# A decoder trunk on one core: the two-operand work of GpSimd moves to VectorE

## The chip, the core and the metric

The kernel runs on one core of a Trainium2 chip. A core has five engines with instruction queues of their own that run in order and wait for each other through semaphores: TensorE (PE in the profile; PEld are its weight loads), VectorE (DVE), ScalarE (ACT), GpSimd (POOL) and SyncE (SP), which here only issues DMA transfers. The metric is the time of one execution on the device in microseconds (us); smaller is better. Before the change the median of three runs is 1664.11 us (1661.08 to 1664.7).

## What is computed

One layer of a hybrid decoder on 1024 tokens of 1024 features, in float32: a mixer with two groups (a causal convolution of width 31 with layer norm, and an RWKV-7 recurrence with 8 heads of 64), cross-attention into 256 memory tokens, and a SwiGLU feed-forward of 2816. Each is wrapped in RMS norms before and after. Cut to the parts that the change touches:

```python
def conformer_conv(u, conv_w, conv_b, ln_g, ln_b):
    h = u[..., :D_CONV] * jax.nn.sigmoid(u[..., D_CONV:])
    h = lax.conv_general_dilated(h, conv_w[:, None, :], window_strides=(1,),
        padding=[(CONV_WIDTH - 1, 0)], ..., feature_group_count=D_CONV) + conv_b
    return jax.nn.silu(layer_norm(h, ln_g, ln_b))

def rwkv7_recurrence(r, w, k, v, kk, a):
    def step(S, inp):
        r_t, w_t, k_t, v_t, kk_t, a_t = inp
        s_kk = jnp.einsum("bhvk,bhk->bhv", S, kk_t)
        S = (S * w_t[:, :, None, :] - s_kk[..., None] * (kk_t * a_t)[:, :, None, :]
             + v_t[..., None] * k_t[:, :, None, :])
        return S, jnp.einsum("bhvk,bhk->bhv", S, r_t)
    ...

def swiglu(h, w_gu, w_down):
    gu = h @ w_gu
    return (jax.nn.silu(gu[..., :D_FF]) * gu[..., D_FF:]) @ w_down
```

## The kernel before

The tokens go through in two blocks of 512, called pass 1 and pass 2 here. Every large product is done in three matmuls (`mm3`, L192): an operand x is split into a rounded part hi and a remainder lo, and hi x hi, hi x lo and lo x hi are summed. Weights come in blocks of 128x1024 (`wload`, L169): SP loads the raw block, ACT rounds it (whi, L166), and DVE or POOL subtracts (wlo, L167). One block feeds 24 matmuls of up to 512 columns. `feat` (psf in the profile) makes feature-major results, `tokmajor` (pst) token-major ones.

The recurrence is done in chunks of 64 tokens, eight to a block. `rwkv_prep` (L417) makes the factors of every head pair. `rwkv_inverse` (L587) inverts unit triangular 64x64 matrices: for the 32x32 diagonal blocks of all chunks and heads at once it takes 31 steps, each a product into tm (L616) and an addition into Tt (L617) over rows 0 to t and columns t+1 to 31. Rows under 20 (`cut`) are POOL's, the others DVE's. Then the result goes through DRAM into TT, and PE completes the blocks (psx, and pst at L643). `rwkv_chain` (L647) goes through the eight chunks one after the other: psp (PE), a copy (ACT), psu (PE), uv (ACT), pss (PE), the new state Sn (DVE, L701) and from it the uv of the next chunk (DVE, L705); psq and psy beside them make the output. After every second chunk `rwkv_out` (L720) normalises it and stores it; the mixing projection (`mix_out`, L809) reads it from DRAM, rounds it (ACT) and subtracts (DVE).

The convolution (`conv_taps`, L336) works on four groups of 128 channels; a tap is one multiply-and-add of 128x512 on DVE (L351), 30 for each group. Group 0 is different: ACT scales the shifted input (tap, L348) and POOL adds (L349).

The convolution and the state chain of a pass stand beside other work for PE: in pass 1 the products of the memory (`memory_maps`, with psgm and psvw) and the input projection of the second block, in pass 2 the feed-forward of the first block. In the source they are generators that are woven together; the order on each engine, however, is made by a scheduler that goes by a timeline of its own and may place an instruction ahead of others wherever its operands allow. Once placed, an engine's queue runs in that order.

In the code the steps of the prediction can be followed at L165 to L182 (lo parts; `pool_share` gives POOL every second or third weight block of some stages), L336 to L354 (taps), L506 to L510 and L547 (three products of the preparation), L607 to L617 (the inverse), L645 (TT), L684 to L713 (the chain), L922 (the last feed-forward's scaling).

Of the kernel before, what the change touches and what calls it, by code (L numbers as in the profile page):

```python
# [9 lines left out]
F32 = mybir.dt.float32  # L10
# [7 lines left out]
P = 128  # L18
# [16 lines left out]
XH = 4  # L35
CONV_ORDER = (1, 2, 0, 3)
CONV_POOL = 0
DECAY = math.exp(-0.5)
# [31 lines left out]
class Trunk:  # L70
    def __init__(self, ctx, tc, x, mem, cols, lora, gpost, w_in, w_out, wqT, wkv, wo, w_gu, w_down, out):
# [92 lines left out]

    def split(self, hi, lo, src, eng=None):  # L165
        self.nc.scalar.copy(out=hi, in_=src)  # L166
        (eng or self.nc.vector).tensor_tensor(out=lo, in0=src, in1=hi.bitcast(F32), op=ALU.subtract)  # L167

    def wload(self, src, k):  # L169

        n = 1024 // k
        raw = self.wp.tile([P, k, n], F32, tag="raw", bufs=4, name="wraw")
        self.nc.sync.dma_start(out=raw, in_=src.rearrange("p (k n) -> p k n", k=k))
        hi = self.wq.tile([P, k, n], F32R, tag="whi", bufs=self.wbufs, name="whi")
        lo = self.wq.tile([P, k, n], F32R, tag="wlo", bufs=self.wbufs, name="wlo")
        self.share += self.pool_share
        eng = None
        if self.share >= 1.0:
            self.share -= 1.0
            eng = self.nc.gpsimd  # L180
        self.split(hi, lo, raw, eng)
        return hi, lo  # L182
# [153 lines left out]
    def conv_taps(self, b, pool, acc):  # L336
        nc = self.nc
        t0 = b * TB
        for j in CONV_ORDER:
            h = pool.tile([P, TB + CONVW - 1], F32, tag="hin", bufs=2, name="hin")  # L340
            nc.sync.dma_start(out=h, in_=self.hd[j * P:(j + 1) * P, t0:t0 + TB + CONVW - 1])
            a = acc[:, j, :]
            w = lambda k: self.cwh[:, j * CONVW + k:j * CONVW + k + 1]
            nc.scalar.activation(out=a, in_=h[:, 0:TB], func=AF.Identity, scale=w(0), bias=self.col("conv_b", j))
            for k in range(1, CONVW):
                if j == CONV_POOL:
                    p = pool.tile([P, TB], F32, tag="t", bufs=2, name="tap")
                    nc.scalar.activation(out=p, in_=h[:, k:k + TB], func=AF.Copy, scale=w(k))  # L348
                    nc.gpsimd.tensor_tensor(out=a, in0=a, in1=p, op=ALU.add)  # L349
                else:  # L350
                    nc.vector.scalar_tensor_tensor(out=a, in0=h[:, k:k + TB], scalar=w(k), in1=a,  # L351
                                                   op0=ALU.mult, op1=ALU.add)
                if k % 6 == 0:
                    yield 4.0  # L354
# [53 lines left out]

    def head_sums(self, hi, lo, src, name, eng=None):

        self.split(hi, lo, src, eng)
        ps = self.pr.tile([P, TB], F32, tag="r", name=name)
        self.nc.tensor.matmul(ps, self.blk, hi, start=True, stop=False)
        self.nc.tensor.matmul(ps, self.blk, lo, start=False, stop=True)
        return ps

    def rwkv_prep(self, b, pool):  # L417
# [74 lines left out]
        def factors(hp, Dx, Di, ta):  # L492
            cl = slice(hp * P, (hp + 1) * P)
            k, n = kk.pop(hp)
            nc.vector.scalar_tensor_tensor(out=n, in0=k, scalar=self.col("k_k", hp), in1=n, op0=ALU.mult, op1=ALU.mult)
            aq = pool.tile([P, 2, NCH, CH], F32, tag="aq", bufs=2, name="aqp")
            bk = pool.tile([P, NCH, 2 * CH], F32, tag="bk", bufs=2, name="bkp")
            nc.vector.tensor_tensor(out=aq[:, 0], in0=c3(n), in1=Dx[:, :, 0:CH], op=ALU.mult)
            nc.vector.scalar_tensor_tensor(out=n, in0=ta, scalar=1.0, in1=n, op0=ALU.add, op1=ALU.mult)
            for g in range(2):  # L500
                nc.vector.scalar_tensor_tensor(out=bk[half[g], :, g * CH:(g + 1) * CH], in0=c3(n)[half[g]],
                                               scalar=0.5, in1=c3(Di)[half[g]], op0=ALU.mult, op1=ALU.mult)
            nc.scalar.activation(out=ta, in_=ta, func=AF.Identity, scale=self.kah[:, hp:hp + 1],
                                 bias=self.kam[:, hp:hp + 1])
            nc.vector.tensor_tensor(out=k, in0=k, in1=ta, op=ALU.mult)
            for g, eng in enumerate((nc.vector, nc.gpsimd)):  # L506
                eng.tensor_tensor(out=bk[half[g], :, (1 - g) * CH:(2 - g) * CH], in0=c3(k)[half[g]], in1=c3(Di)[half[g]],
                                  op=ALU.mult)
            r = load(hp, "r")
            nc.gpsimd.tensor_tensor(out=aq[:, 1], in0=c3(r), in1=Dx[:, :, 1:CH + 1], op=ALU.mult)  # L510
            nc.sync.dma_start(out=self.qd[cl, c0:c0 + NCH, :], in_=aq[:, 1])
            nc.vector.scalar_tensor_tensor(out=r, in0=r, scalar=self.col("r_k", hp), in1=k, op0=ALU.mult, op1=ALU.mult)
            return aq, bk, r, ta

        def products(hp, aq, bk, r, gt):
# [30 lines left out]
            hl = pool.tile([P, 2, TB], F32R, tag="rt", name="bhl")  # L546
            nc.vector.tensor_tensor(out=v, in0=self.head_sums(hl[:, 0, :], hl[:, 1, :], r, "psbk", nc.gpsimd), in1=v, op=ALU.mult)  # L547

# [38 lines left out]
    def rwkv_inverse(self, b, pool, TT):  # L587
# [18 lines left out]

        cut = 20  # L607
        for t in range(31):
            for eng, r0, r1 in ((nc.gpsimd, 0, min(cut, t + 1)), (nc.vector, cut, t + 1)):
                n, m = r1 - r0, 31 - t  # L610
                if n <= 0:
                    continue
                a = At[:, t, t + 1:32].unsqueeze(1).broadcast_to([P, n, m])
                c = Tt[:, r0:r1, t].unsqueeze(2).broadcast_to([P, n, m])
                w, u = tm[:, r0:r1, 0:m], Tt[:, r0:r1, t + 1:32]
                eng.tensor_tensor(out=w, in0=a, in1=c, op=ALU.mult)  # L616
                eng.tensor_tensor(out=u, in0=u, in1=w, op=ALU.add)  # L617
        nc.sync.dma_start(out=self.sc2[b], in_=Tt)
# [282 lines left out]
    def ffn(self, hT, ya, ss, pool):  # L901
# [3 lines left out]
        def down(acts, f0):  # L905
# [4 lines left out]
            def sink(t, half, ps):  # L910
# [6 lines left out]
                if last:  # L917
                    nc.scalar.activation(out=self.junk()[:, 0:TB], in_=y, func=AF.Square,
                                         accum_out=ss[t][:, half:half + 1])
                    if half == 0:  # L920
                        self.half_mean(ss[t])
                    eng = nc.gpsimd if half == 1 and t < 2 else nc.vector  # L922
                    eng.tensor_tensor(out=y, in0=y, in1=gb[:, c], op=ALU.mult)
            yield from self.tokmajor(self.w_down, acts, 4, sink, 2 if last else 1, f0)
# [25 lines left out]
    def run(self):  # L950
# [177 lines left out]
```

## Time and profile before

| | us |
|---|---|
| median of 3 runs | 1664.11 |
| the profiled execution | 1665.11 |
| its span, from the first to the last instruction | 1663.4 |
| PE busy | 1562.1 |
| DVE busy | 1055.0 |
| ACT busy | 722.0 |
| POOL busy | 368.7 |

The page gives each engine's busy time, and the span in 40 equal slices (41.6 us each) with one digit for each engine: the busy share in tenths. PEclk is the granted clock of TensorE in tenths of its full 2.4 GHz. Matmuls are pipelined, so the duration of one is longer than the distance to the next. The same is so, by less, on DVE. Where PE's row shows 9, PE is the bound and the others have room; where it falls, another engine or a wait sets the pace.

### The profile page before, as it was taken

The numbers are of one execution on the slowest core, as the hardware profiler recorded it, in microseconds if no ns is written. First come the engines' busy times: TensorE is split into PE (matmuls) and PEld (weight loads), VectorE is DVE, ScalarE is ACT, GpSimd is POOL, SyncE is SP. The second block draws the span as 40 slices with busy tenths as digits, with TensorE's granted clock in tenths as the row PEclk, the third lists the DMA queues.
The fourth block names the chain that finished last, engine by engine and source line by source line (L and its number), as shares of the span: only waits on it lengthen the run. The fifth ranks groups of instructions, "written<-read, shape, count | busy, mean of one in ns | idle before, by whom it ended". The sixth has DMA issues, their size and how long they took to land.

```text
span 1663.4 us, 22818 instructions
## 1 busy us (share of the span) xinstructions
PE 1562.1 (94%) x8688; PEld 1257.0 (76%) x8688; DVE 1055.0 (63%) x1501; ACT 722.0 (43%) x1122; POOL 368.7 (22%) x344
## 2 busy tenths in 40 slices
PE   7999866879999999999979889999999999999997
PEld 6777855767787888777757667777887788888886
DVE  5677698997545546768789996636537624343435
ACT  5654335867434434664224556524435232222222
POOL 1032390740000001022561730012113211111111
PEclk9999976889999999999999899999999999999999
DMA  6576967466636336457844335445236532323221
GB/s 206 166 223 190 283 203 220 127 196 216 234 117 203 95 100 192 139 165 210 252 119 141 96 114 161 157 126 204 87 91 229 214 102 89 102 89 101 89 89 51
DMA packets 175644, 257.37 MB, mean 155 GB/s; under 512 B 68912, under 2 KB 110000, under 8 KB 175536
## 3 DMA queue, kind: packets, MB, share of 16 engines
q1 hardware_dynamic: 174576, 255.08, 49.4%
q8 instruction: 68, 1.11, 0.3%
q10 hardware_dynamic: 960, 0.85, 0.2%
q14 instruction: 40, 0.33, 0.1%
HBM read 196.58 MB, written 59.31 MB: 154 GB/s over the span
## 4 chain that ended last, share of the span: by engine, by line
PE 46%; DVE 4%; POOL 4%; issue 2%; DMA 1%; ACT 0%; SPq 0%; POOLq 0%; DVEq 0%; ACTq 0%
PE psf L196 8%; PE psf L195 7%; PE psf L194 7%; PE pst L194 7%; PE pst L195 7%; PE pst L196 7%; DVE acc L351 2%; POOL Tt L617 1%; POOL tm L616 1%; PE psg L523 1%; DVE wlo L167 1%; DMA At<-sc 0%; PE pstr L274 0%; DMA btd<-bt 0%; POOL rstd L234 0%
## 5 line engine op out<-in xcount | busy, mean ns | idle before, releaser
L166 ACT CAST whi<-wraw 128x1024 fp32r<-128x1024 f32 x256 | 267.5, 1047 | 556.8 <-PE psf L195 222.7
L196 PE MATMUL psf<-ahi,wlo 128*128 128x512 f32 (+1 forms) x1200 | 468.7, 391 | 24.6 <-DVE wlo L167 23.5
L194 PE MATMUL psf<-ahi,whi 128*128 128x512 f32 (+1 forms) x1200 | 465.3, 389 | 9.6 <-ACT whi L166 9.4
L195 PE MATMUL psf<-alo,whi 128*128 128x512 f32 (+1 forms) x1200 | 465.1, 388 | 0.0
L167 DVE TENSOR_TENSOR wlo<-wraw,whi 128x1024 fp32r<-128x1024 f32 x223 | 284.7, 1278 | 268.4 <-ACT whi L166 266.7
L196 PEld LDWEIGHTS psf<-ahi,wlo 128*128 128x128 f32 x1200 | 232.3, 194 | 77.0 <-DVE wlo L167 29.2
L194 PEld LDWEIGHTS psf<-ahi,whi 128*128 128x128 f32 x1200 | 232.8, 194 | 58.8 <-ACT whi L166 11.8
L195 PEld LDWEIGHTS psf<-alo,whi 128*128 128x128 f32 x1200 | 232.9, 194 | 48.0 <-issue 1.2
L167 POOL TENSOR_TENSOR wlo<-wraw,whi 128x1024 fp32r<-128x1024 f32 x33 | 79.7, 2414 | 566.1 <-ACT whi L166 508.0
L351 DVE SCALAR_TENSOR_TENSOR acc<-hin,cols,acc 128x512 f32<-128x512 f32 x180 | 165.0, 945 | 0.7
L195 PE MATMUL pst<-wlo,ahi 128*128 128x512 f32 x384 | 152.2, 396 | 0.9 <-POOL wlo L167 0.9
L196 PE MATMUL pst<-whi,alo 128*128 128x512 f32 x384 | 150.5, 397 | 0.0
L194 PE MATMUL pst<-whi,ahi 128*128 128x512 f32 x384 | 137.3, 399 | 2.7 <-ACT ahi L277 2.1
L195 PE MATMUL pst<-wlo,fhi 128*128 128x512 f32 x352 | 138.8, 395 | 0.0
L196 PE MATMUL pst<-whi,flo 128*128 128x512 f32 x352 | 135.3, 393 | 0.0
L194 PE MATMUL pst<-whi,fhi 128*128 128x512 f32 x352 | 135.0, 396 | 0.0
L234 POOL TENSOR_TENSOR rstd<-rstd,mhalf 128x1 f32<-128x1 f32 x50 | 34.1, 689 | 394.1 <-DVE rstd L233 385.6
L349 POOL TENSOR_TENSOR acc<-acc,tap 128x512 f32<-128x512 f32 x60 | 97.1, 1618 | 87.5 <-ACT tap L348 84.1
L916 DVE TENSOR_TENSOR ya<-pst,ya 128x512 f32<-128x512 f32 x80 | 54.2, 686 | 53.5 <-PE pst L196 53.4
L194 PEld LDWEIGHTS pst<-whi,ahi 128*128 128x128 f32 x384 | 71.7, 188 | 20.1 <-ACT ahi L277 2.6
L195 PEld LDWEIGHTS pst<-wlo,ahi 128*128 128x128 f32 x384 | 72.1, 188 | 18.2 <-POOL wlo L167 1.2
L196 PEld LDWEIGHTS pst<-whi,alo 128*128 128x128 f32 x384 | 71.8, 188 | 16.6
(241 smaller groups left out, 2004.0 us busy)
## 6 DMA issues: line engine op xcount, KB each, us to landing
wraw<-in_w_gu_dram SPq DMA_DIRECT2D x88, 512.0 KB, 3.7
wraw<-in_w_in_dram SPq DMA_DIRECT2D x44, 512.0 KB, 4.5
wraw<-in_w_down_dram SPq DMA_DIRECT2D x44, 512.0 KB, 3.6
wraw<-in_wkv_dram SPq DMA_DIRECT2D x16, 512.0 KB, 5.4
am<-amd SPq DMA_DIRECT2D x16, 512.0 KB, 5.5
wraw<-in_w_out_dram SPq DMA_DIRECT2D x16, 512.0 KB, 4.1
wraw<-gd SPq DMA_DIRECT2D x16, 512.0 KB, 4.0
wraw<-vwd SPq DMA_DIRECT2D x16, 512.0 KB, 3.4
```

Of the source, the lines that this page charges most:

```text
L166: self.nc.scalar.copy(out=hi, in_=src)
L167: (eng or self.nc.vector).tensor_tensor(out=lo, in0=src, in1=hi.bitcast(F32), op=ALU.subtract)
L194: mm(ps, w[0], x[0], start=start, stop=False)
L195: mm(ps, w[0], x[1], start=False, stop=False)
L196: mm(ps, w[1], x[0], start=False, stop=stop)
L234: nc.gpsimd.tensor_tensor(r, r, self.mhalf, op=ALU.pow)
L349: nc.gpsimd.tensor_tensor(out=a, in0=a, in1=p, op=ALU.add)
L351: nc.vector.scalar_tensor_tensor(out=a, in0=h[:, k:k + TB], scalar=w(k), in1=a, op0=ALU.mult, op1=ALU.add)
L523: nc.tensor.matmul(pg[g][:, i, :], bk[half[g], c + i, :], aq[half[g], :, c + i, :], start=True, stop=True)
L616: eng.tensor_tensor(out=w, in0=a, in1=c, op=ALU.mult)
L617: eng.tensor_tensor(out=u, in0=u, in1=w, op=ALU.add)
L916: nc.vector.tensor_tensor(out=y, in0=ps, in1=y, op=ALU.add)
```

## The change

POOL keeps its constants, the tiny rstd powers and copies; everything large with two operands goes to DVE. The taps of group 0 become multiply-and-add like the others, and ACT's scaled copies for them go away. The groups are taken in the order 0 to 3. The inverse is one product and one addition per step over all rows. All lo parts, `bkp` and `aqp` of the preparation and the last scaling are DVE's.

```diff
     def split(self, hi, lo, src):
         self.nc.scalar.copy(out=hi, in_=src)
-        (eng or self.nc.vector).tensor_tensor(out=lo, in0=src, in1=hi.bitcast(F32), op=ALU.subtract)
+        self.nc.vector.tensor_tensor(out=lo, in0=src, in1=hi.bitcast(F32), op=ALU.subtract)
...
-        self.share += self.pool_share
-        eng = None
-        if self.share >= 1.0:
-            self.share -= 1.0
-            eng = self.nc.gpsimd
-        self.split(hi, lo, raw, eng)
+        self.split(hi, lo, raw)
...
-        for j in CONV_ORDER:
+        for j in range(4):
...
-                if j == CONV_POOL:
-                    p = pool.tile([P, TB], F32, tag="t", bufs=2, name="tap")
-                    nc.scalar.activation(out=p, in_=h[:, k:k + TB], func=AF.Copy, scale=w(k))
-                    nc.gpsimd.tensor_tensor(out=a, in0=a, in1=p, op=ALU.add)
-                else:
-                    nc.vector.scalar_tensor_tensor(out=a, in0=h[:, k:k + TB], scalar=w(k), in1=a,
-                                                   op0=ALU.mult, op1=ALU.add)
+                nc.vector.scalar_tensor_tensor(out=a, in0=h[:, k:k + TB], scalar=w(k), in1=a,
+                                               op0=ALU.mult, op1=ALU.add)
...
-            for g, eng in enumerate((nc.vector, nc.gpsimd)):
-                eng.tensor_tensor(out=bk[half[g], :, (1 - g) * CH:(2 - g) * CH], in0=c3(k)[half[g]], in1=c3(Di)[half[g]],
-                                  op=ALU.mult)
+            for g in range(2):
+                nc.vector.tensor_tensor(out=bk[half[g], :, (1 - g) * CH:(2 - g) * CH], in0=c3(k)[half[g]], in1=c3(Di)[half[g]],
+                                        op=ALU.mult)
             r = load(hp, "r")
-            nc.gpsimd.tensor_tensor(out=aq[:, 1], in0=c3(r), in1=Dx[:, :, 1:CH + 1], op=ALU.mult)
+            nc.vector.tensor_tensor(out=aq[:, 1], in0=c3(r), in1=Dx[:, :, 1:CH + 1], op=ALU.mult)
...
-            nc.vector.tensor_tensor(out=v, in0=self.head_sums(hl[:, 0, :], hl[:, 1, :], r, "psbk", nc.gpsimd), in1=v, op=ALU.mult)
+            nc.vector.tensor_tensor(out=v, in0=self.head_sums(hl[:, 0, :], hl[:, 1, :], r, "psbk"), in1=v, op=ALU.mult)
...
-        cut = 20
         for t in range(31):
-            for eng, r0, r1 in ((nc.gpsimd, 0, min(cut, t + 1)), (nc.vector, cut, t + 1)):
-                n, m = r1 - r0, 31 - t
-                ...
-                eng.tensor_tensor(out=w, in0=a, in1=c, op=ALU.mult)
-                eng.tensor_tensor(out=u, in0=u, in1=w, op=ALU.add)
+            n, m = t + 1, 31 - t
+            ...
+            nc.vector.tensor_tensor(out=w, in0=a, in1=c, op=ALU.mult)
+            nc.vector.tensor_tensor(out=u, in0=u, in1=w, op=ALU.add)
...
-                    eng = nc.gpsimd if half == 1 and t < 2 else nc.vector
-                    eng.tensor_tensor(out=y, in0=y, in1=gb[:, c], op=ALU.mult)
+                    nc.vector.tensor_tensor(out=y, in0=y, in1=gb[:, c], op=ALU.mult)
...
-        self.pool_share = 0.5
...
-        self.pool_share = 0.0
...
-        self.pool_share = 0.3
```

Since the scheduler goes by what it takes each operation to cost, the order changes as well. On DVE before, in pass 1, the last of its own inverse rows (L616, L617) are followed at once by taps (L351, into acc) and lo parts of weights (wlo); POOL's rows are on POOL's queue:

```order
L616 TENSOR_TENSOR tm<-At,Tt 128x10x2
L617 TENSOR_TENSOR Tt<-Tt,tm 128x10x2
L616 TENSOR_TENSOR tm<-At,Tt 128x11
L617 TENSOR_TENSOR Tt<-Tt,tm 128x11
L351 SCALAR_TENSOR_TENSOR acc<-hin,cols,acc 128x512 x2
L583 TENSOR_TENSOR vt<-psv,vm 128x512
L351 SCALAR_TENSOR_TENSOR acc<-hin,cols,acc 128x512 x3
L583 TENSOR_TENSOR vt<-psv,vm 128x512
L351 SCALAR_TENSOR_TENSOR acc<-hin,cols,acc 128x512
L167 TENSOR_TENSOR wlo<-wraw,whi 128x1024
```

On DVE now, in the same pass, in the middle of the inverse (its product is L598 and its addition L599, taps are L337, lo parts L163, and kvl at L811 the memory's lo parts):

```order
L163 TENSOR_TENSOR wlo<-wraw,whi 128x1024
L599 TENSOR_TENSOR Tt<-Tt,tm 128x14x18
L811 TENSOR_TENSOR kvl<-psf,kvh 128x256
L337 SCALAR_TENSOR_TENSOR acc<-hin,cols,acc 128x512 x2
L163 TENSOR_TENSOR wlo<-wraw,whi 128x1024
L811 TENSOR_TENSOR kvl<-psf,kvh 128x256
L598 TENSOR_TENSOR tm<-At,Tt 128x15x17
L337 SCALAR_TENSOR_TENSOR acc<-hin,cols,acc 128x512 x2
L163 TENSOR_TENSOR wlo<-wraw,whi 128x1024
L599 TENSOR_TENSOR Tt<-Tt,tm 128x15x17
L337 SCALAR_TENSOR_TENSOR acc<-hin,cols,acc 128x512 x2
```

From the tenth step of the inverse on, every one of its operations is followed by two taps, and many by a lo part, until its 31st step. On PE before, in pass 1, the seventh step of the chain has matmuls of the input projection (psf) within it:

```order
L684 MATMUL psp<-uv,am 64x64 x8
L196 MATMUL psf<-ahi,wlo 128x512
L194 MATMUL psf<-ahi,whi 128x512
L195 MATMUL psf<-alo,whi 128x512
L196 MATMUL psf<-ahi,wlo 128x512
L194 MATMUL psf<-ahi,whi 128x512
L689 MATMUL psq<-qt,Sn 64x64 x8
L195 MATMUL psf<-alo,whi 128x512
L196 MATMUL psf<-ahi,wlo 128x512
L194 MATMUL psf<-ahi,whi 128x512
```

On PE now, in the same pass, steps of the chain follow each other (psp is L666, psq L671, psu L676, pss L681, psy L691; psbs, at L399 and L400, belongs to the normalisation of a finished pair of chunks):

```order
L666 MATMUL psp<-uv,am 64x64 x8
L671 MATMUL psq<-qt,Sn 64x64 x8
L676 MATMUL psu<-pt,TT 64x64 x8
L681 MATMUL pss<-uv,bt 64x64
L691 MATMUL psy<-am,uv 64x64
L681 MATMUL pss<-uv,bt 64x64 x7
L691 MATMUL psy<-am,uv 64x64 x7
L399 MATMUL psbs<-yhl,blk 128x512
L400 MATMUL psbs<-yhl,blk 128x512
L666 MATMUL psp<-uv,am 64x64 x8
L671 MATMUL psq<-qt,Sn 64x64 x8
```

The psf blocks that stood there are ahead of the chain now: the last five of the eight steps of pass 1, and the last six of pass 2, have no other matmuls between them.

## Rows read from the trace of the kernel before

**Rows 1.** The page: the span, busy time, and 40 slices of PE and its clock.
```profile
span 1663.4 us, 22818 instructions
...
PE 1562.1 (94%) x8688; PEld 1257.0 (76%) x8688; DVE 1055.0 (63%) x1501; ACT 722.0 (43%) x1122; POOL 368.7 (22%) x344
...
PE   7999866879999999999979889999999999999997
...
PEclk9999976889999999999999899999999999999999
```

**Rows 2.** Busy time by stage: stretch, length, each engine's busy us, clock, DMA share, GB/s.
```profile
196.00:251.00 55.00, 36.67 (x235) 32.55 (x233) 50.64 (x74) 17.62 (x26) 49.03 (x62) 0.84 0.69 221
...
275.00:365.00 90.00, 69.46 (x682) 60.91 (x679) 85.94 (x105) 57.54 (x102) 49.77 (x32) 0.79 0.52 163
...
811.00:862.00 51.00, 42.72 (x186) 33.38 (x184) 47.51 (x73) 10.07 (x12) 46.33 (x60) 1.00 0.51 170
...
905.00:980.00 75.00, 62.01 (x417) 48.26 (x417) 71.70 (x69) 42.06 (x64) 49.30 (x30) 0.89 0.38 114
...
1300.00:1640.00 340.00, 340.00 (x1471) 275.77 (x1470) 133.94 (x145) 92.02 (x115) 43.56 (x18) 1.00 0.30 94
```

**Rows 3.** Groups of POOL's instructions: count, busy us, mean ns, idle before and releaser.
```profile
L349 POOL TENSOR_TENSOR acc<-acc,tap 128x512 f32<-128x512 f32 x60 | 97.1, 1618 | 87.5 <-ACT tap L348 84.1
L167 POOL TENSOR_TENSOR wlo<-wraw,whi 128x1024 fp32r<-128x1024 f32 x33 | 79.7, 2414 | 566.1 <-ACT whi L166 508.0 <-DMA pdr<-evq 41.8 <-issue 16.2
L617 POOL TENSOR_TENSOR Tt<-Tt,tm 128x60 f32<-128x60 f32 (+24 forms) x62 | 49.1, 792 | 4.9
L616 POOL TENSOR_TENSOR tm<-At,Tt 128x60 f32<-128x60 f32 (+24 forms) x62 | 46.8, 754 | 13.2 <-DMA At<-sc 5.5 <-PE psv L577 3.0
```

**Rows 4.** Timeline of DVE, pass 1: start, us for all, instruction and count.
```profile
272.51 6.71 DVE L351 SCALAR_TENSOR_TENSOR acc<-hin,cols,acc 128x512 f32<-128x512 f32 x10
...
321.21 1.22 DVE L167 TENSOR_TENSOR wlo<-wraw,whi 128x1024 fp32r<-128x1024 f32 x1
322.35 0.42 DVE L829 TENSOR_TENSOR kvl<-psf,kvh 128x256 fp32r<-128x256 f32 x1
322.68 3.94 DVE L351 SCALAR_TENSOR_TENSOR acc<-hin,cols,acc 128x512 f32<-128x512 f32 x3
```

**Rows 5.** Timeline of the chain's first step in pass 1, to the second psp.
```profile
275.41 1.12 PE L684 MATMUL psp<-uv,am 128*64 128x64 f32 x16
...
276.46 1.12 PE L689 MATMUL psq<-qt,state 64*64 64x64 f32 x16
...
278.83 0.68 PE L694 MATMUL psu<-pt,TT 64*64 64x64 f32 x16
...
280.90 0.63 PE L709 MATMUL psy<-am,uv 128*64 128x64 f32 x13
...
282.96 0.42 DVE L701 TENSOR_TENSOR Sn<-pss,state 128x256 f32<-128x256 f32 x1
...
285.01 0.87 DVE L705 TENSOR_TENSOR uv<-Sn,dc 64x256 f32<-64x256 f32 x2
...
285.53 1.52 PE L684 MATMUL psp<-uv,am 128*64 128x64 f32 x16 [3.99 <-issue]
```

**Rows 6.** Timeline: the inverse's first operation in pass 1; its first matmuls in pass 2.
```profile
196.85 0.24 POOL L616 TENSOR_TENSOR tm<-At,Tt 128x31 f32<-128x31 f32 x1 [3.02 <-PE psv L577]
...
873.45 2.23 PE L636 MATMUL psx<-X,TT 32*32 32x32 f32 x128
```

**Rows 7.** Timeline, end of pass 2: last psy, last product, first matmuls of the projection.
```profile
1051.63 0.64 PE L709 MATMUL psy<-am,uv 128*64 128x64 f32 x16
...
1070.85 0.69 DVE L737 TENSOR_TENSOR Y<-Y,bv 128x512 f32<-128x512 f32 x1
...
1081.12 1.01 PE L194 MATMUL pst<-whi,ahi 128*128 128x512 f32 x2 [0.48 <-DVE ya L916]
```

**Rows 8.** Timeline, end of pass 1: the first matmuls of the projection.
```profile
449.67 0.62 PE L194 MATMUL pst<-whi,ahi 128*128 128x512 f32 x2
```

More of the change, by code (lines that the diff above doesn't have):

```diff
@@ L35 @@
 XH = 4
-CONV_ORDER = (1, 2, 0, 3)
-CONV_POOL = 0
 DECAY = math.exp(-0.5)
@@ L131, in __init__ @@
         self.lbh = derive("lbh", 4, col("ln_b"), 0.5, 0.0)
-        self.pool_share = self.share = 0.0
         self.state = cp.tile([P, HP, HD], F32, tag="state", bufs=2, name="state0")
@@ L162, in col, with split @@
         return self.cols[:, a:b] if i is None else self.cols[:, a + i:a + i + n]
-    def split(self, hi, lo, src, eng=None):
+    def split(self, hi, lo, src):
         self.nc.scalar.copy(out=hi, in_=src)
-        (eng or self.nc.vector).tensor_tensor(out=lo, in0=src, in1=hi.bitcast(F32), op=ALU.subtract)
+        self.nc.vector.tensor_tensor(out=lo, in0=src, in1=hi.bitcast(F32), op=ALU.subtract)
     def wload(self, src, k):
@@ L407, in lora_split, with head_sums @@
                                     op=ALU.subtract)
-    def head_sums(self, hi, lo, src, name, eng=None):
-        self.split(hi, lo, src, eng)
+    def head_sums(self, hi, lo, src, name):
+        self.split(hi, lo, src)
         ps = self.pr.tile([P, TB], F32, tag="r", name=name)
@@ L605, in rwkv_inverse @@
         nc.gpsimd.memset(tf[:, 0:1024:33], 1.0)
-        cut = 20
         for t in range(31):
-            for eng, r0, r1 in ((nc.gpsimd, 0, min(cut, t + 1)), (nc.vector, cut, t + 1)):
-                n, m = r1 - r0, 31 - t
[L611 to L615, printed above, removed]
-                eng.tensor_tensor(out=w, in0=a, in1=c, op=ALU.mult)
-                eng.tensor_tensor(out=u, in0=u, in1=w, op=ALU.add)
+            n, m = t + 1, 31 - t
+            a = At[:, t, t + 1:32].unsqueeze(1).broadcast_to([P, n, m])
+            c = Tt[:, 0:n, t].unsqueeze(2).broadcast_to([P, n, m])
+            w, u = tm[:, 0:n, 0:m], Tt[:, 0:n, t + 1:32]
+            nc.vector.tensor_tensor(out=w, in0=a, in1=c, op=ALU.mult)
+            nc.vector.tensor_tensor(out=u, in0=u, in1=w, op=ALU.add)
         nc.sync.dma_start(out=self.sc2[b], in_=Tt)
```

## The prediction

> **What bounds the kernel now.** I read the page first, then busy time by stage, then the order of the instructions, then pieces of the timeline. TensorE (PE) is busy for 1562.1 us of the span of 1663.4, VectorE (DVE) for 1055.0 and GpSimd (POOL) for 368.7 [rows 1]. Over most of the span PE is full and nothing another engine does can count: in 1300 to 1640 it is busy for all of 340 us with 1471 matmuls, so 0.231 us for one of 512 columns [rows 2]. The reader is to see the two holes, in slices 5 to 9 and 21 to 24 of the page, where PE's row falls to 6 and its granted clock with it [rows 1]. They are the two passes of inverse, convolution and state chain. In 275 to 365 DVE is busy 85.94 of 90 us, PE 69.46 at a mean granted clock of 0.79 (a mix of its two levels, 1.2 and 2.4 GHz); in 905 to 980 DVE 71.70 of 75 [rows 2]. In these stretches DVE's queue sets the pace, and POOL's long additions run beside it. So the change has to be judged by what it does to DVE's queue in two stretches of together some 450 us.
>
> **What moves, and its price.** POOL loses 60 tap additions (97.1 us), 33 lo parts (79.7) and 124 inverse operations (49.1 + 46.8) [rows 3], and 28 smaller products of the preparation and the last sub-layer. On DVE the prices are these. A tap costs 0.67: ten in a row took 6.71 with POOL idle. With POOL adding beside it three took 3.94, so 1.31 each. A lo part of 128x1024 is followed by the next instruction after 1.14 (321.21 to 322.35), a 256-wide operation after 0.33 [rows 4]. One of 512 shows 0.69 and one of 256 0.42 [rows 4, 7], so 1.05 ns per element, and after the overlap with the next instruction some 0.07 us fixed. An inverse has 31 steps of a product and an addition on (t+1)(31-t) elements, 10,912 in all: 62 x 0.07 + 11.5 = 15.8 us on DVE if nothing came between, against a run on POOL that fills 49.03 of the 55 us from 196 to 251 and 46.33 of the 51 from 811 to 862 [rows 2].
> So per stretch DVE takes over 30 x 0.67 + 15.8 = 36 us, drops its own share of the inverse rows, and is rid of about 0.64 us on each of some 30 taps that ran against POOL: near zero. ACT loses 60 scaled copies, but with 57.54 of 90 us busy it did not set the pace there [rows 2]. The lo parts and the smaller products fall where PE is full (preparation, last feed-forward): 33 x 1.14 us more on a DVE that is busy 133.9 of 340 us in 1300 to 1640 [rows 2]. I cost them at nothing; the cover is PE's own 5.5 us per weight block (24 matmuls x 0.231), and even without it a lo part on DVE is shorter than on POOL (1.14 for 2.41). Short waits of PE on POOL's lo parts and scales go; I take -3 us, between -6 and 0.
>
> The Trainium skill ("SBUF — State Buffer", section "Who interferes with whom") says that a VectorE instruction with two SBUF inputs and a GpSimd one that reads SBUF exclude each other, the later one waiting for the whole of the first. The trace agrees, 0.67 against 1.31 us per tap. By that rule alone the move would be free or a gain, which is the first rival below.
>
> **What decides is the order.** The scheduler places the inverse's operations one by one among the other work of DVE: between two of them stand two taps and often a lo part, and that through the whole inverse, in both passes. Before, POOL ran its share in one piece. On DVE's queue the first pass of the inverse now holds, from its first to its last operation, 77 taps (51.6), 24 lo parts (27.4), 12 operations of 256 columns (4.0), 16 residues of the transposes (6.6), its own 15.8 and 5 of small ones: 110 us. DVE kept at most 0.92 to 0.955 of such stretches busy (50.64 of 55, 85.94 of 90) [rows 2]; with 0.94 that is 117 us, so the inverse, which starts at 196.85 [rows 6], ends at about 314, not at 251. Bounds: 307 with no idle time, 326 with 0.85.
> The state chain of eight steps begins only after that. Before, its steps stood among memory maps and feed-forward blocks; now most of those blocks stand ahead of it in PE's queue. Between the last steps PE has nothing else: five steps in pass 1, six in pass 2, and then the mixing projection waits for the last chunk. The order shown with the change has a piece of each.
>
> **An uncovered step.** The trace has none quite bare; the nearest is the first, 10.1 us from psp at 275.41 to the next psp at 285.53, with transposes ahead of psu and taps ahead of the state [rows 5]. Its own parts are psp 1.12, psq 1.12, psu to the end of psy 2.7 (278.83 to 281.53), the new state 0.42 and its copies 0.87: 6.2 us. To that comes, every second step, the normalisation of a finished chunk on ACT and DVE, which stands in both queues between the step's own instructions. I take 8; the bounds are 6, the bare parts, and 11, the step as the trace has it and 1 us for loads that come late.
>
> **The uncovered tail.** From the last psy at 1051.63 to the last product of that chunk 1070.85 and the first matmul of the projection at 1081.12 took 29.5 us, with feed-forward work beside it [rows 7]. ACT's queue now has all eight roundings of the projection's input ahead of its first weight, so PE waits for the tail whole. Without the rest some 4 us fall away: 25, bounds 20 and 28.
>
> **The sum.** Pass 1: 314, then ten weight blocks (10 x 5.5) and about 12 us of small matmuls of the inverse and the three covered steps, 69 us with 2 us lag, 385; 5 x 8 = 40, 425; 25, 450; and 3 for the lower clock after idling: 453. Before, the projection began at 449.67 [rows 8]: +3. Bounds: 307 + 69 + 30 + 20 = 426 and 326 + 77 + 55 + 28 = 486, -24 and +36.
> Pass 2: from 811 on PE has 30 weight blocks before the inverse's matmuls, 30 x 5.5 = 167, and DVE about 150 us beside them; with 9 us of mutual waits the inverse's matmuls begin near 987. Before it was 873.45 [rows 6]; little is lost by that alone, since PE works. Then 34 us of covered work and 6 of waits, 1027; 6 x 8 = 48, 1075; 25, 1100; 3 for the clock: 1103. Before it began at 1081.12 [rows 7]: +22. The PE work up to that place is the same in both. Bounds: 982 + 34 + 36 + 20 = 1072 and 1000 + 40 + 66 + 28 = 1134, -9 and +53.
> Together +3 + 22 - 3 = +22. The profiled execution took 1665.11 (its span and 1.7 around it), 1.0 above the median: 1687 on its scale, 1686 on the median's. A measurement of this kernel can tell about 0.2%, 3.3 us, from no change.
>
> **Rivals.** (1) Faster: the end of POOL's contention decides. If an uncovered step costs the bare 6 and the tail 20, pass 1 ends 10 to 20 us earlier than before (DVE's queue is through with the convolution some 20 us sooner) and pass 2 about level. The point from which it decides is a step of 6 us with a tail of 25: then the +22 of the eleven steps is gone. For it: taps at 0.67 instead of 1.31, and PE's loss of 8.3 us in 811 to 862 [rows 2, 4]. Against it: in both passes the chain no longer has a cover. It gives about 1650. That is also where the rule of the Trainium skill's page would lead. (2) Much slower: steps paced by their loads. A step's loads go through SP's one queue, in order, behind stores of finished chunks that wait for DVE; at 11 us a step and not 8 that is 11 x 3 = 33 us more, 1720. (3) Level, within 3 us: the two cancel, 1664.
>
> **Chances.** My forecast, 1670 to 1705 with the middle at 1686: 0.60. Rival 1: 0.18. Rival 2: 0.14. Rival 3: 0.08. Slower by over 0.2% is the forecast and rival 2, 0.74; same 0.08; faster 0.18. The range of 8 in 10 reaches into both sides, 1648 to 1732.
>
> **What would show it.** POOL's busy time falls to under 60 us; DVE's total changes by little (60 x 0.67 + 33 x 1.14 + 2 x 15.8 and the small ones, about 115 us more, less some 95 of contention), and the mean of a tap falls from 0.945 to near 0.7. The inverse's operations span about 117 and 165 us on DVE. PE's row shows two new holes, near 385 to 450 and 1030 to 1100, with the granted clock at its lower level, while the old holes fill. After 1110 all is as before, later by the sum. I am wrong if the holes are shorter than about 45 us (step of 6), or if the inverse ends well before 300.

## The result, and the profile after

The changed kernel takes 1683.39 us (median of 4 runs, 1681.95 to 1686.29) against 1663.87 for the kernel before on the same chips: a ratio of 1.0123, 95% interval 1.0104 to 1.0141. It is slower by 20 us; 22 were forecast. The profiled execution has a span of 1684.6 us. The page of after, to be held against [rows 1]:

```profile
span 1684.6 us, 22643 instructions
...
PE 1561.7 (93%) x8688; PEld 1258.4 (75%) x8688; DVE 1065.0 (63%) x1702; ACT 687.4 (41%) x1062; POOL 50.5 (3%) x99
...
PE   6999876998599999999999997589999999999998
...
PEclk9999997999599999999999999589999999999999
```

The old holes are smaller: slices 5 to 9 read 8 7 6 9 9 where they read 8 6 6 8 7, and slices 21 to 24 are full. Two new ones stand in slices 10 to 11 and 25 to 27, with the granted clock at half in slices 11 and 26. DVE's total has hardly changed (1055.0 to 1065.0) and PE's not at all; the place of the waits has.

Busy time by stage of after (columns as in [rows 2]): the inverse of pass 1, three covered steps of the chain, the bare steps, the end of pass 1, the inverse of pass 2, the bare steps with the tail of pass 2, and the rest:

```profile
203.00:325.00 122.00, 89.69 (x562) 77.66 (x561) 113.45 (x210) 55.86 (x88) 1.97 (x2) 0.85 0.70 227
340.00:400.00 60.00, 60.00 (x683) 46.48 (x682) 50.23 (x79) 34.64 (x53) 0.00 (x0) 1.00 0.55 182
400.00:442.00 42.00, 26.65 (x406) 22.22 (x405) 21.49 (x43) 22.25 (x40) 0.00 (x0) 0.70 0.55 167
437.00:464.00 27.00, 13.69 (x70) 10.01 (x71) 13.09 (x21) 12.35 (x19) 0.00 (x0) 0.50 0.24 75
823.00:980.00 157.00, 156.37 (x680) 126.21 (x678) 149.08 (x251) 41.10 (x50) 0.00 (x0) 1.00 0.42 130
1035.00:1101.00 66.00, 35.33 (x489) 29.01 (x489) 33.20 (x64) 33.88 (x58) 0.00 (x0) 0.62 0.46 139
1110.00:1660.00 550.00, 545.31 (x2399) 441.04 (x2398) 260.19 (x360) 177.13 (x274) 17.37 (x20) 1.00 0.37 120
```

In the inverse's stretches DVE is nearly full (113 of 122 us, 149 of 157) and in pass 2 PE is full too. Then, at 400 and again at 1035, no engine is full: PE waits for a chain of short steps. DVE at the end of the inverse of pass 1 (timeline, columns as in [rows 4]):

```profile
318.86 1.22 DVE L163 TENSOR_TENSOR wlo<-wraw,whi 128x1024 fp32r<-128x1024 f32 x1
320.00 1.40 DVE L337 SCALAR_TENSOR_TENSOR acc<-hin,cols,acc 128x512 f32<-128x512 f32 x2
321.32 0.21 DVE L598 TENSOR_TENSOR tm<-At,Tt 128x31 f32<-128x31 f32 x1
321.45 1.21 DVE L163 TENSOR_TENSOR wlo<-wraw,whi 128x1024 fp32r<-128x1024 f32 x1
322.58 1.40 DVE L337 SCALAR_TENSOR_TENSOR acc<-hin,cols,acc 128x512 f32<-128x512 f32 x2
323.91 0.21 DVE L599 TENSOR_TENSOR Tt<-Tt,tm 128x31 f32<-128x31 f32 x1
```

The last step of the inverse is two operations of 0.21 us, and takes 2.8 us (321.32 to 324.12), because two taps and a lo part stand between them. Not every pair of operations has two taps between, as the part on the change has it for the later steps: of the 61 gaps in pass 1 34 hold two, 9 one and 18 none, 77 taps in all. And a bare step, on PE, from one psp to the next (to be held against [rows 5]):

```profile
400.33 0.39 PE L187 MATMUL psf<-ahi,wlo 128*128 128x512 f32 x1
400.65 0.69 PE L666 MATMUL psp<-uv,am 128*64 128x64 f32 x16
401.27 0.68 PE L671 MATMUL psq<-qt,Sn 64*64 64x64 f32 x16
403.70 0.68 PE L676 MATMUL psu<-pt,TT 64*64 64x64 f32 x16 [1.75 <-ACT pt L667]
404.86 0.33 PE L681 MATMUL pss<-uv,bt 128*64 128x64 f32 x2 [0.48 <-ACT uv L678]
...
408.53 0.24 PE L666 MATMUL psp<-uv,am 128*64 128x64 f32 x1 [2.12 <-issue]
```

After 400.65 no matmul of another kind follows until the projection, but for the two of psbs that belong to each finished pair of chunks. A step takes 7.9 us here, and PE works some 3.5 us of it.

### The profile page after: what moved, and what is told of

It is laid out like the page before. It is cut to its first block, busy times and chain, and to the rows that moved or that the text cites. A ratio compares the mean times of both kernels' runs of the same rounds, so it can differ in the third digit from the quotient of the medians.

```text
span 1684.6 us, 22643 instructions
## 1 busy us (share of the span) xinstructions
PE 1561.7 (93%) x8688; PEld 1258.4 (75%) x8688; DVE 1065.0 (63%) x1702; ACT 687.4 (41%) x1062; POOL 50.5 (3%) x99
## 5 line engine op out<-in xcount | busy, mean ns | idle before, releaser
L163 DVE TENSOR_TENSOR wlo<-wraw,whi 128x1024 fp32r<-128x1024 f32 x256 | 313.1, 1224 | 294.3 <-ACT whi L162 291.3
L187 PE MATMUL psf<-ahi,wlo 128*128 128x512 f32 (+1 forms) x1200 | 463.3, 387 | 7.2 <-DVE wlo L163 7.1
L185 PE MATMUL psf<-ahi,whi 128*128 128x512 f32 (+1 forms) x1200 | 459.3, 384 | 7.3 <-ACT whi L162 4.4
L185 PEld LDWEIGHTS psf<-ahi,whi 128*128 128x128 f32 x1200 | 228.7, 191 | 56.3 <-ACT whi L162 6.2
L186 PEld LDWEIGHTS psf<-alo,whi 128*128 128x128 f32 x1200 | 228.8, 191 | 48.0 <-issue 1.2
L337 DVE SCALAR_TENSOR_TENSOR acc<-hin,cols,acc 128x512 f32<-128x512 f32 x240 | 171.7, 751 | 1.8 <-ACT acc L335 1.6
L186 PEld LDWEIGHTS pst<-wlo,fhi 128*128 128x128 f32 x352 | 66.1, 188 | 15.2 <-DVE wlo L163 0.4
L185 PEld LDWEIGHTS pst<-whi,fhi 128*128 128x128 f32 x352 | 65.8, 188 | 15.2 <-ACT whi L162 0.4
L187 PEld LDWEIGHTS pst<-whi,flo 128*128 128x128 f32 x352 | 66.1, 188 | 14.7
```

What stands on the lines that cost most here:

```text
L163: self.nc.vector.tensor_tensor(out=lo, in0=src, in1=hi.bitcast(F32), op=ALU.subtract)
L185: mm(ps, w[0], x[0], start=start, stop=False)
L186: mm(ps, w[0], x[1], start=False, stop=False)
L187: mm(ps, w[1], x[0], start=False, stop=stop)
```

## How the runs were read

Three readings stand for each run beside its time. **The inverse**: from its first to its last operation. **Bare steps**: steps of the chain, of eight in each pass, that hold under 1.05 us of other matmuls (psbs aside). **Lost time of PE**: the length of a stretch less its matmuls, each counted at the pace that it has where PE is full (0.233 us for 512 columns, 0.117 for 256, 0.065, 0.045 and 0.04 for 128, 64 and 32). Every kernel here issues the same 8688 matmuls, 1490 us by this count, so what is lost is what differs. The three readings are of the profiled execution, the times are medians; run 4's profiled execution (1626.65) lies 3.5 us under its median. Pass 1 is counted from the first psv (the transposes of the values, ahead of the inverse) to the first transpose of the attention's probabilities (pspt), pass 2 from 780 us to that transpose of the second block.

| kernel | us | ratio to before, 95% | inverse, pass 1, 2 | bare steps | lost in pass 1 | lost in pass 2 |
|---|---|---|---|---|---|---|
| before | 1663.9 | | 53.8, 51.6 | 2, 0 | 77.4 | 35.1 |
| after | 1683.4 | 1.0104 to 1.0141 | 120.6, 156.0 | 5, 6 | 88.9 | 50.3 |
| 1 inverse alone | 1695.2 | 1.016 to 1.021 | 108.7, 129.5 | 4, 3 | 93.6 | 50.1 |
| 2 after, inverse back | 1637.9 | 0.9816 to 0.9856 | 52.8, 53.1 | 1, 0 | 70.4 | 19.8 |
| 3 after, taps behind | 1636.7 | 0.9808 to 0.9857 | 43.6, 47.4 | 0, 0 | 73.6 | 18.2 |
| 4 taps alone | 1630.2 | 0.9771 to 0.9813 | 53.8, 51.6 | 2, 0 | 64.5 | 11.8 |
| 5 lo parts alone | 1657.2 | 0.9952 to 0.9978 | 52.5, 53.2 | 1, 0 | 78.0 | 33.7 |
| 6 as 1, taps behind | 1642.9 | 0.9866 to 0.9899 | 43.4, 44.5 | 0, 0 | 71.7 | 20.6 |
| 7 taps + inverse, behind | 1636.0 | 0.9821 to 0.985 | 42.5, 45.5 | 0, 0 | 67.8 | 16.3 |
| 8 as 4, idle additions | 1676.2 | 1.0068 to 1.0098 | 52.6, 52.6 | 2, 0 | 87.4 | 41.0 |
| 9 after, 30 taps free | 1639.1 | 0.9828 to 0.9861 | 68.5, 77.7 | 2, 1 | 68.6 | 21.9 |
| 10 after, 60 taps free | 1662.6 | 0.9986 to 1.0007 | 101.4, 113.6 | 4, 3 | 84.6 | 32.0 |
| 11 as 4, shared anew | 1636.7 | 0.9815 to 0.9848 | 41.2, 43.3 | 1, 0 | 65.1 | 18.7 |
| 12 as 4, idle copies | 1645.7 | 0.9881 to 0.9915 | 53.6, 52.8 | 2, 0 | 71.3 | 22.4 |

Where both engines hold parts of the inverse (before, 2, 4, 5, 8, 11 and 12), its length is POOL's.

## The experiments

Theory O is the prediction's: the order costs, since the inverse's operations are threaded through DVE's queue and the chain behind them stands uncovered. Theory L: the sheer load on DVE costs. Theory C: contention of POOL and DVE is what decides.

**1. The inverse alone, and 6. the same with the taps behind it.** The kernel before with `cut = 20` and POOL's rows gone; in run 6 in addition

```diff
-                    nc.vector.scalar_tensor_tensor(out=a, in0=h[:, k:k + TB], scalar=w(k), in1=a, ...)
+                    with self.tc.issue_after(self.inv_last):
+                        nc.vector.scalar_tensor_tensor(out=a, in0=h[:, k:k + TB], scalar=w(k), in1=a, ...)
```

where `inv_last` is the inverse's last addition: the taps follow it in DVE's queue, and nothing waits for it to finish.

> The kernel before with the inverse alone moved to VectorE; the taps of group 0, the lo parts and the small products stay where they were. Theory O (the order costs: the inverse is threaded one operation at a time through DVE's queue, and the state chain then stands uncovered): in the order the inverse stretches here over 184 DVE instructions in pass 1 and 200 in pass 2, some 105 and 125 us, and three to four steps of the chain in each pass have no other matmuls. So nearly the whole loss comes with this part alone: 1675 to 1690, the inverse's first to last operation over 95 us in both passes. Theory L (the load: DVE was full in these stretches, and what is added to it, 115 us in all, is what costs): this part is 32 of the 115 us, so a third of the loss, about 1670. Theory C (contention: POOL beside DVE is what costs, and taking it away can only help): POOL's long run from 196 to 251 goes, so 1650 to 1660.

> The kernel with the inverse alone moved to DVE (1695 measured), with one thing more: DVE's taps are queued behind the last operation of the same pass's inverse, in issue order only. Theory O (order): the inverse takes about 40 us and not 109 and 130, the chain is covered in every step, and the 31 us are won back: 1650 to 1668. Theory L (load): same work on DVE, 1685 to 1700.

Run 1 took 1695.2 us, 31 more than before, worse than the whole change and 5 above Theory O's range. Run 6 took 1642.9. Both have the same operations on the same engines; DVE is busy 1064.9 and 1068.9 us in them. Some 50 us lie in the order alone: some 31 undo the loss, and the rest is a gain of 19 us over before, more than Theory O had expected (1650 to 1668). Not all of run 1's longer inverse is threading: four of its operations in pass 1 and seven in pass 2 met one of POOL's additions and took 1.0 to 1.1 us more each (last section), 4 of its 109 us and 7 of its 130. Theory L as stated falls, and Theory C too (1650 to 1660 for run 1).

**2. The change with the inverse back, and 3. with the taps behind it.** Run 2 has before's split of the rows, run 3 the two lines of run 6.

> The changed kernel with the inverse alone put back as before (rows under 20 on POOL, the others on DVE); taps, lo parts and small products stay on DVE. Theory O: the inverse is a block on POOL again, over in about 52 us, every step of the chain has 7 to 15 us of other matmuls beside it, and the loss is gone; with the taps at 0.67 us and not 1.31 it is faster than before: 1645 to 1658. Theory L: 84 of the 115 us of added DVE work are still there, so about two thirds of the loss: 1675 to 1680. Theory C: near 1655, since only the inverse runs beside DVE.

> The changed kernel with one thing more: every tap of the convolution is queued on DVE behind the last operation of the same pass's inverse (issue order only, no wait is added). All operations and engines are those of the changed kernel. Theory O: the inverse then has 10 lo parts and a few small ones between its 62 operations, about 35 us in pass 1 and 45 in pass 2 instead of 120.6 and 156.0; it ends at about 240 and 870, the chain is covered in every step, and most of the two holes of PE closes: 1605 to 1645, faster than both. Theory L: DVE has the same work in the same stretch, so 1675 to 1690 as the changed kernel. Theory C: as the changed kernel, since POOL is idle in both.

1637.9 and 1636.7, the first faster than any theory had it: either way of taking the taps out of the inverse is worth 46 us against after, and turns the loss into a gain of 26 and 27. In run 3 the edit changes nothing but the place of the taps, and POOL has no part in the inverse, so Theory C, which had it level with after, falls as well. DVE at the end of the inverse of pass 1, run 3:

```profile
244.39 0.22 DVE L599 TENSOR_TENSOR tm<-At,Tt 128x60 f32<-128x60 f32 x1
244.64 0.22 DVE L600 TENSOR_TENSOR Tt<-Tt,tm 128x60 f32<-128x60 f32 x1
244.90 0.22 DVE L599 TENSOR_TENSOR tm<-At,Tt 128x31 f32<-128x31 f32 x1
245.02 0.48 DVE L269 SCALAR_TENSOR_TENSOR alo<-pstr,cols,ahi 128x256 fp32r<-128x256 f32 x1
245.42 0.21 DVE L600 TENSOR_TENSOR Tt<-Tt,tm 128x31 f32<-128x31 f32 x1
245.54 1.41 DVE L338 SCALAR_TENSOR_TENSOR acc<-hin,cols,acc 128x512 f32<-128x512 f32 x2
```

It ends at 245.6 instead of 324.1. No step of the chain is bare then, and its last psy ends at 402. The rest of the hoped-for gain (1605 to 1645 was expected, and the upper half came) is lost to the convolution, which is now last. The end of pass 1 in run 3, ACT, DVE, SP's store and PE:

```profile
432.88 1.02 SPq L380 DMA_DIRECT2D yd<-acc  x2
435.15 1.40 DVE L379 SCALAR_TENSOR_TENSOR acc<-lnth,acc 128x512 f32<-128x512 f32 x2 [1.58 <-ACT acc L378]
435.67 0.37 SPq L730 DMA_DIRECT2D araw<-yd  x1
436.13 0.89 SPq L380 DMA_DIRECT2D yd<-acc  x2
439.99 1.14 ACT L162 CAST ahi<-araw 128x512 fp32r<-128x512 f32 x2 [4.16 <-DMA araw<-yd]
...
440.66 0.80 PE L185 MATMUL pst<-whi,ahi 128*128 128x512 f32 x1 [17.01 <-ACT ahi L162]
```

PE waits 17.0 us for the first rounded input of the projection, and that comes from the convolution (the load at 435.67 stands behind the store at 432.88), not from the chain. Theory L holds for what is left only up to the last tap, which ends at 400: from 250 until then DVE is busy 139 of 150 us. Of the 41 us that follow (engines as in [rows 2]) DVE is busy 25.7 and PE 16.8:

```profile
400.00:441.00 41.00, 16.75 (x90) 11.65 (x89) 25.68 (x43) 24.80 (x33) 0.00 (x0) 0.73 0.34 117
```

The convolution's layer norm is a chain of short steps too, and it now stands uncovered in the chain's place. DVE's load decides when it begins, not how long it lasts.

**9 and 10. How many taps in between.** As run 3, with the first 30 or 60 taps of a pass left free:

```diff
-                with self.tc.issue_after(self.inv_last):
+                with self.tc.issue_after(self.inv_last if j * 30 + k > 30 else self.inv_first):
```

> The changed kernel with the taps of groups 1 to 3 queued behind the inverse and the 30 of group 0 left free: 30 taps stand between the inverse's operations in each pass, where the changed kernel has 78 and 101, and the run with all taps behind has none (1637). Theory O: the inverse takes some 75 to 85 us, one or two steps of the chain stand bare in the order of PE, so a loss of 1 or 2 steps of 8 us and a little more against 1637: 1640 to 1655. If it is the sheer number of operations on DVE (Theory L) the time is that of the changed kernel or of the run with all behind, with no row between them.

> As the run with 30 free taps, with 60 of them free in each pass. Theory O: the inverse takes 105 to 125 us, three to four steps of each pass stand bare: 1656 to 1676, between the run with 30 and the changed kernel.

1639.1 (0.9 under Theory O's range) and 1662.6 (within it), between 1636.7 without any and 1683.4 with 77 and 100 (the expectation's 78 and 101 count the tap behind the last operation). The inverse takes 44, 69, 101, 121 us in pass 1 (75 to 85 and 105 to 125 were expected for runs 9 and 10) and the bare steps are 0, 2, 4, 5; in pass 2 47, 78, 114, 156 and 0, 1, 3, 6. The first 30 cost 2 us, within the spread, so run 9 alone doesn't part Theory O from Theory L; run 10 does. In run 9 the projection starts at 435.8, in run 3 at 440.7, since the chain, now ending at 421, still ends before the convolution (434). From there on it is the chain that ends last: 23 us for the next 30 taps and 21 for the rest. The 23 us of run 10 lie a little above what the 4 more bare steps hold by themselves (some 5 us of waiting each).

**4. The taps alone, 8. with idle additions on POOL, 12. with idle copies.** Run 4 is the kernel before with group 0 on DVE. Runs 8 and 12 add to it

```diff
+                if j == 2:
+                    nc.gpsimd.tensor_tensor(out=nz[:, 0, :], in0=h[:, k:k + TB], in1=nz[:, 1, :], op=ALU.add)
```

or, in run 12, `nc.gpsimd.tensor_copy(out=nz[:, 0, :], in_=h[:, k:k + TB])`; nz is read by nobody.

> The kernel before with the 60 taps of group 0 alone moved to DVE (and the groups taken 0 to 3). Theory O: the inverse stays a block on POOL and the chain stays covered, so no loss: 1650 to 1664. Theory L: 40 of the 115 us of added DVE work, a third of the loss: about 1671. Theory C: POOL's additions at 275 to 365 and 905 to 980 go, the taps there fall from 1.31 to 0.67 us, PE gains what it lost there: 1645 to 1655.

> The kernel with the taps alone moved to DVE (1630 measured), with 60 additions of 128x512 on POOL added again, 30 in each pass, with the same input as taps of group 2 and a result that nobody reads: POOL is as busy beside DVE as before, and nothing waits for it. Theory C (the additions on POOL slowed DVE's taps, and that was the cost of group 0 on POOL): the taps beside them rise from 0.74 to 1.1 to 1.3 us, 15 to 25 us in each pass, and the time to 1650 to 1680. If the gain of moving the taps came from elsewhere (the 60 scaled copies of ACT, the order of the groups, the wait for group 0's chain of additions): 1627 to 1635.

> As the run with 60 idle additions on POOL (1676), with one-operand copies of 128x512 in their place: same order on PE, same input read. Theory C in its strict form (whatever POOL reads from SBUF excludes a two-input operation of DVE for as long as it lasts): the copies make the taps beside them wait too, by one copy each, so 30 copies cost per pass what they last, and the time is between 1645 and 1676. If only POOL's two-operand work disturbs: 1628 to 1640, as the run without idle work (1630).

1630.2, 1676.2 and 1645.7. Run 4 gained more than any theory had expected (1645 at best); run 8 came where Theory C put it, and run 12 at the low end of its range. Groups of DVE and POOL, of runs 4, 8 and 12 in this order (columns as on the page: count, busy us, mean ns, idle before):

```profile
L346 DVE SCALAR_TENSOR_TENSOR acc<-hin,cols,acc 128x512 f32<-128x512 f32 x240 | 180.6, 789 | 0.8 <-ACT acc L344 0.4
```

```profile
L348 DVE SCALAR_TENSOR_TENSOR acc<-hin,cols,acc 128x512 f32<-128x512 f32 x240 | 210.1, 913 | 0.7 <-ACT acc L346 0.3
L351 POOL TENSOR_TENSOR nz<-hin,nz 128x512 f32<-128x512 f32 x60 | 91.5, 1526 | 58.1 <-DMA hin<-hd 53.5
```

```profile
L348 DVE SCALAR_TENSOR_TENSOR acc<-hin,cols,acc 128x512 f32<-128x512 f32 x240 | 190.8, 831 | 0.7 <-ACT acc L346 0.3
L351 POOL COPY nz<-hin 128x512 f32<-128x512 f32 x60 | 56.1, 934 | 56.1 <-DMA hin<-hd 52.5
```

Sixty additions that nobody waits for cost 46 us. DVE's busy time rises from 1043.0 to 1087.8, 44.8 us, of which 29.5 are on the taps and the rest on other operations beside them. So the gain of moving the taps is the end of contention: 46 us given back, for 14 that the move costs otherwise (run 8 against before, both with POOL's additions running). No share of ACT's 60 scaled copies is needed to explain it; a small one within the 14 isn't excluded, since they are gone in runs 4 and 8 alike. The copies cost 15.6 us, DVE's busy time rises by 13.5; both by a third of the additions' price, at 0.93 against 1.53 us of POOL's time each.

The Trainium skill ("SBUF — State Buffer", section "Who interferes with whom") states that a VectorE operation with two SBUF inputs contends with a GpSimd one that reads SBUF. Run 8 agrees by operand: the 40 taps beside an addition took 1.47 us in the mean and the 200 others 0.80, while an alo<-pstr, with one of its two tensors in PSUM, took 0.47 beside the additions and 0.48 elsewhere. Run 12 agrees in kind, 36 taps beside a copy at 1.03 us. Three of these operations beside POOL's additions, run 8:

```profile
302.21 0.47 DVE L278 SCALAR_TENSOR_TENSOR alo<-pstr,cols,ahi 128x256 fp32r<-128x256 f32 x1
302.61 1.37 DVE L348 SCALAR_TENSOR_TENSOR acc<-hin,cols,acc 128x512 f32<-128x512 f32 x1
303.90 0.47 DVE L278 SCALAR_TENSOR_TENSOR alo<-pstr,cols,ahi 128x256 fp32r<-128x256 f32 x1
301.82 3.11 POOL L351 TENSOR_TENSOR nz<-hin,nz 128x512 f32<-128x512 f32 x2
```

**5. The lo parts and small products alone.** `pool_share` at 0.0 throughout, and the 28 products on DVE.

> The kernel before with the lo parts and the 28 small products of the preparation and the last sub-layer alone moved to DVE; taps of group 0 and the inverse stay as before. The prediction's own step (these fall where PE is full and cost nothing, and short waits on POOL go): 1658 to 1664. Theory P (the preparation is bound by DVE's queue for some blocks, and each operation moved there delays it: with the lo parts on DVE the first psv stands at 199.5 to 200.6, without at 193.1 to 196.1): 4 to 7 us later at the end of the preparation and about as much again in pass 2, so 1668 to 1677.

1657.2 us, a gain of 5.8 (ratio 0.9965, 0.9952 to 0.9978) and just under the range of the prediction's step (1658): nearly all outside the two passes, as that step has it. Theory P was a misreading: the first psv comes 2.5 us later in run 5 than before, but more matmuls stand ahead of it (165 us of work against 159 by the count above), and no time is lost.

**7. Taps and inverse behind, lo parts as before, and 11. the rows shared anew.** Run 7 is run 6 with the taps of group 0 on DVE. Run 11 is run 4 with `cut = 12` and the taps behind DVE's last row.

> Taps and inverse on DVE, lo parts and small products as before, and the taps queued behind the inverse: the run with all work on DVE and taps behind (1637) less the lo parts. With the order mended DVE is what bounds pass 1 from 200 to 437, so Theory L holds for what is left: the inverse on DVE costs 32 us of DVE and takes away the contention beside it (about 12 + 7 us), so 1628 to 1638, no better than the run with the taps alone (1630). If the earlier start of the chain counts by itself (259.6 against 269.2), 1615 to 1628.

> The kernel with the taps alone moved (1630), with the inverse shared out anew: POOL takes rows under 12 instead of 20, DVE the others, and the taps are queued behind DVE's last operation of the inverse, so that DVE's rows stay together. If the start of the chain still costs something when the order is mended, the inverse on POOL gets shorter (about 40 us instead of 53) and the chain starts 10 us sooner: 1615 to 1628. If DVE's load bounds pass 1 (Theory L for what is left), DVE has 10 us more per pass and the time is 1628 to 1640.

1636.0 and 1636.7: no better than run 4, though the chain's first psp comes sooner (265.7 and 263.2 against 272.9). The convolution's last result of pass 1 stands at 432.3 and 431.0, against 422.4 in run 4, and the projection starts at 436.3, 434.0 and 433.1. An earlier chain buys nothing there. That it is the added work on DVE which keeps them behind run 4 is argued and not shown: PE loses 3.3 and 0.6 us more than in run 4 in pass 1, 4.5 and 6.9 more in pass 2. Run 4, the taps alone, is the best of all: 2.1% faster than before and 3.2% faster than after (1630.2 against 1683.4).

## Why the prediction was right, step by step

The sum was 22 us; 20 were measured. Its mechanism is shown by runs 1, 3, 6 and 10. Of its terms some were off, and they cancelled, so that it came within 2 us is in part luck. In pass 1 the inverse ended 10 us late, the covered stretch up to 400.65 took 5.5 more and the steps 2 more than forecast; the tail and the clock took 18 less before the projection began.

**The inverse on DVE.** Forecast 117 us with DVE 0.94 busy; measured 120.6 with 112.4 busy, 0.93, with 77 taps and 24 lo parts between, as forecast. It began 6.7 us later than before, with more matmuls ahead of it, so it ended at 324.1 and not 314, still within the bounds of 307 to 326. In pass 2 156.0 us (about 150 and 165 were named), its matmuls at 994.4 instead of 987.

**The bare steps.** Five and six were forecast, five and six came. From 400.65 to the end of the last psy at 442.4 are 41.8 us, 8.4 each; in pass 2 from 1035.5 to 1087.6, 8.7 each: 8 was taken. By turns they are short (6.9 to 7.9) and long (8.8 to 11.0), since ACT has the normalisation of a finished pair in most of the long ones (416.84 to 421.76 in the step from 415.94), as the prediction had it.

**The tail was mis-sized.** 25 us were forecast (20 to 28); the projection began 10.3 us after the last psy in pass 1 and 13.4 in pass 2. The end of pass 1 in after, PE:

```profile
441.32 1.11 PE L691 MATMUL psy<-am,uv 128*64 128x64 f32 x13
445.34 0.79 PE L399 MATMUL psbs<-yhl,blk 128*128 128x512 f32 x1 [2.91 <-ACT yhl L162]
...
452.75 0.79 PE L185 MATMUL pst<-whi,ahi 128*128 128x512 f32 x1 [5.89 <-ACT ahi L162]
453.35 0.63 PE L186 MATMUL pst<-wlo,ahi 128*128 128x512 f32 x1
...
459.02 1.22 PE L187 MATMUL pst<-whi,alo 128*128 128x512 f32 x2 [2.48 <-DVE alo L163]
```

The step that failed is "so PE waits for the tail whole". The projection takes the convolution's features first, and those had been stored by 395. Of them only the first rounding (452.10) and its eight products stood ahead of the chain's last results, behind the chain's normalisation in ACT's queue. The wait at 459.02 is for the remainder of that first block: it and the next three roundings (458.27 and 458.31) waited, by the profile, for the store of the chain's last output. The chain's own features are rounded at 461.91 and 464.69 and multiplied from 470.8 on, with no wait. So a part of the tail was still waited for; that buffers of the projection stand where the chain's were would fit, but no run shows it. What the projection gained in its start it partly gave back: its matmuls follow each other at 0.43 us (453.35, 453.77) and not 0.233 while the granted clock is 0.50 until 464, at the lower of its two levels after the waits. With the wait of 2.48 that is another 6.8 us lost between 452.75 and 470, where 3 were put down for the clock.

**The two passes.** Pass 1: +3 forecast, +11.5 lost (88.9 against 77.4): the later inverse and the clock. Pass 2: +22 forecast, +15.2 lost: the shorter tail. Both are within their bounds. The starts of the projection, 452.75 and 1100.92, agree with the forecast 453 and 1103 more closely than the terms do. The second of them hides a slip: it was reckoned as if pass 2 still began at 811, though pass 1's delay goes ahead of it; at 780 PE had lost 5.5 us more than before.

**Elsewhere.** -3 forecast (-6 to 0); -5.5 lost (the span's 21.2 less the two passes), most of it in the preparation of the second block (11.3 to 6.8). From 1110 on PE is full (545.31 of 550), and from the second pspt to the end are 484.5 us where before had 483.9: no term there, as said.

**The signs named in advance.** POOL 50.5 us (under 60 named), DVE's total up by 10.0 (20 named), the new holes at 400 to 464 and 1035 to 1105 (385 to 450 and 1030 to 1100 named). The mean of a tap fell from 0.945 to 0.751, not 0.7, which is the distance and not the duration of one:

```profile
L337 DVE SCALAR_TENSOR_TENSOR acc<-hin,cols,acc 128x512 f32<-128x512 f32 x240 | 171.7, 751 | 1.8 <-ACT acc L335 1.6
```

**The rivals.** Rival 1 named a real force and undersold it. The end of contention is worth 46 us for the taps alone, and without the threading the change would have been 27 us faster than before (run 3), 13 beyond its 1650. It lost because the order costs 46 at the same time; the prediction had the net of the two, not their sizes. Rival 2, steps paced by loads at 11 us, did not come: 8.4 and 8.7 a step. Rival 3, level, came only in run 10, with 60 taps between.

**What stays open.** The parts do not add up: taps alone -34, inverse alone +31, lo parts alone -6 make -9, and the change is +20. Some of it is clear, since the taps of group 0 lengthen the inverse further (108.7 and 129.5 to 120.6 and 156.0, from 4 and 3 bare steps to 5 and 6), but no run split the rest. Nor was it tried to let the scheduler know the true prices, or to give PE's queue back its cover while the inverse stays threaded.

## What to carry to other kernels

When a long chain of short operations goes to a busy engine, count what the scheduler puts between its links, not the chain's own time: operations whose own durations add up to 21 us (62 of 0.34) took 121 and 156, and what waits behind it on another engine loses its cover. Look at the order before moving work, and hold independent work back behind the chain if it has slack; here that one line was worth 46 us. Measure a suspected contention with idle work that nobody waits for, and move first the part that contends most and depends least: the taps alone were the best version.

## What the runs showed of the hardware that was not expected

A one-operand copy on POOL disturbs DVE too, by a third as much as a two-operand addition of the same size: 15.6 against 46 us for 60, or 0.17 against 0.49 us more on the taps per POOL instruction (10.2 and 29.5 us over 60). The inverse's short operations suffer as well, and not evenly: an addition into Tt took 438 ns in the mean in run 1, in run 6 340, and that is the work of a few. Of the 124 operations of the inverse in run 1 the eleven that met one of POOL's additions took 1.29 to 1.40 us, 1.0 to 1.1 more than the same step in run 6, whatever their size; the others are equal within 0.02.

```profile
L613 DVE TENSOR_TENSOR Tt<-Tt,tm 128x31 f32<-128x31 f32 (+15 forms) x62 | 27.2, 438 | 0.4
```

```profile
L614 DVE TENSOR_TENSOR Tt<-Tt,tm 128x31 f32<-128x31 f32 (+15 forms) x62 | 21.1, 340 | 1.2
```

One such step, the addition of 87 columns, in run 1 with the POOL addition beside it, and in run 6:

```profile
297.84 1.32 DVE L613 TENSOR_TENSOR Tt<-Tt,tm 128x87 f32<-128x87 f32 x1
297.29 1.76 POOL L349 TENSOR_TENSOR acc<-acc,tap 128x512 f32<-128x512 f32 x1 [0.76 <-ACT tap L348]
```

```profile
236.55 0.25 DVE L614 TENSOR_TENSOR Tt<-Tt,tm 128x87 f32<-128x87 f32 x1
```

The short operation began 0.55 us after POOL's and ended 0.11 us after it.
